# Where the last-state products of three head groups stand in a hybrid decoder layer

## The chip, the cores and the metric

The kernel runs on one core of a Trainium2 chip. The core has a matrix engine (TensorE, PE in the profile, with its weight loads as PEld), three engines for elementwise work (VectorE or DVE, ScalarE or ACT, GpSimd or POOL) and SyncE (SP), which only starts transfers here. Each engine takes its instructions from a queue of its own, in an order fixed when the program is built, and waits where an operand isn't ready. The metric is the device time of one execution in microseconds (us).

## The reference

One inference step of a layer with two halves, in float32, for 256 new prompt positions and 8 sequences of 8 sampled positions each (320 tokens, which are the columns of nearly every tile here):

```python
x = x + rms_post(W_out @ [chunkMLP(h) || SSD(h)])    # h = rms_pre(x)
x = x + rms_post(ConvFFN(rms_pre(x)))                # D_MODEL 2048, D_FF 5632
```

SSD is a state-space mixer of 32 heads in 4 groups. The prompt is handled in two chunks of 128 tokens. The state of a group after the prompt (128 state columns by 8 heads of 64) is one of the outputs, `ssm_state_prompt`, and nothing else reads it:

```python
states = einsum("bcsgn,bcsgr,bcsgrp->bcgrpn", bc, decay_states, xdt)       # one per chunk
new_states = einsum("bzcgr,bcgrpn->bzgrpn", chunk_decay, [init, *states])
states_in, final = new_states[:, :-1], new_states[:, -1]                   # final: the output
```

For each group the last state is thus a decayed state of chunk 0 plus a product of chunk 1: the tokens' B columns times the decayed inputs.

## The kernel before, in words

**Products.** Activations lie transposed, 128 features on the partitions and 320 tokens along the row. To hold float32 accuracy, each operand is split into a rounded part and a rest (`hi`, `lo`), and a product is made of three: `whi` with `xhi`, `whi` with `xlo`, `wlo` with `xhi` (`accumulate`, L141 to L143). Weights come in slabs of 512 KB: SP loads `wraw`, ACT casts it to `whi` (L128), DVE subtracts to get `wlo` (L130), with three buffers of each.

**Stages.** (1) the first norm and the projections by `w_in`, group by group, with the gated MLP and the four SSD groups beside them; (2) `w_out`, chunk by chunk, added into `acc_mix` by DVE (`chunk_out`, L234), each chunk right after the group that feeds it; (3) the second norm: the post-norm of the first half, the residual, and the pre-norm of the FFN; (4) the FFN's up and down products in eleven groups of 512 columns, with its convolution, and beside it the renewal of the sampled sequences' states (`renewals`); (5) the last norm.

**Order.** The program is written as Python generators. The work of the SSD groups and the renewals are tasks that advance to their next `yield` each time a weight slab has been used (`tick`). A scheduler then lays out each engine's queue by priority: `first()` and `high_priority` move instructions ahead, `tc.issue_after(x)` keeps them behind x. Where a task stands in the text is therefore not always where its instructions stand on an engine.

**An SSD group** (`ssd`, L774 on): `decayed(i, c)` (L818) has POOL multiply the inputs of chunk c by their decay, into tile `xde`; a product with chunk 0's B gives `s1_ps`, copied by ACT into `s1` (L835); DVE and ACT make the decay factors (`decays`, from sums `cs` that SP loads again from DRAM); `products` makes the outputs of the heads, in pairs (`y_ps`, L902); then POOL decays `s1` (L924). The inner function `final` (L927 on) makes the last state: a product of 128x512 in float32 (`fin_ps`, L929, `x1d` being chunk 1's decayed inputs), DVE's sum `s1 + ps` (L931), and the out DMA (L932). For groups 0 to 2 this is done at the end of the group, with the DMA on ACT's queue. For group 3 it is kept back in `rest`: its product and its sum are placed in the second norm, and its DMA goes out on POOL's queue.

**The second norm** (L1002 on). While the last chunk of `w_out` is being added, `squares_of` (L302) squares each of the 16 blocks of `acc_mix` as it becomes final and adds the squares up: ACT squares and POOL adds up to block 12; block 13's square goes to PSUM (`sq_ps`) and is added by DVE; blocks 14 and 15 have squares of their own. `root_table` (L271) has ACT load its table for the square root ahead of use, by a root of a constant; it stands behind the square of block 12. PE sums the squares over the partitions (`token_sums`, L282, three calls), `rsqrt_by_root` (L259) makes 1/root from the sums with one root on ACT, and `spread` (L290) brings the result into all partitions through PE. Between the sums and `spread` stands the last-state product of group 3. Behind `spread`, `unread` (L1005) issues eleven products of 128x320 whose results nobody reads.

`x1_ready` (L1038) then handles the 16 blocks in turn: DVE multiplies by the norm (L1043) and adds the residual (L1044), and `split` makes `h_hi` on ACT (L368) and `h_lo` on DVE (L369). The FFN's first `project` runs beside it, with six accumulators at a time: `ps_0` to `ps_3` in the four banks `mm`, and two more in banks of `misc`.

**The renewals** (L1150 on) begin with six empty steps, one per FFN weight slab.

Of the kernel before, what the change touches and what calls it, by code (L numbers as in the profile page):

```python
# [9 lines left out]
F32 = mybir.dt.float32  # L10
F32R = mybir.dt.float32r
I32 = mybir.dt.int32
AF = mybir.ActivationFunctionType
ALU = mybir.AluOpType
# [3 lines left out]
P = 128  # L18
# [3 lines left out]
NT = NP + NS  # L22
D = 2048
KD = D // P
# [10 lines left out]
def hybrid_step(  # L35
# [9 lines left out]
    nc = tc.nc  # L45
    act, dve, pool, pe, sp = nc.scalar, nc.vector, nc.gpsimd, nc.tensor, nc.sync
# [3 lines left out]
    cp = ctx.enter_context(tc.tile_pool(name="cp", bufs=1))  # L50
# [6 lines left out]
    def misc(name):  # L57
        return ms.tile([P, 512], F32, tag="ms", name=name)
# [6 lines left out]
    with tc.high_priority(offset=300000):  # L65
        dve.memset(ones, 1.0)

        ps = misc("early")
# [34 lines left out]
    def col(i):  # L103
        return prm[:, i:i + 1]


    def first():

        return tc.high_priority(offset=200000)
# [109 lines left out]
    acc = None  # L219
# [51 lines left out]
    def root_table(behind):  # L271

        there = tp.tile([P, 1], F32, tag="there", name="root_there", bufs=1)
        with tc.issue_after(behind):
            act.activation(there, ones[:, 0:1], AF.Sqrt)

    def token_sums(sq, ps=None, more=False):

        begins = ps is None
        ps = misc("tsum") if begins else ps  # L280
        for c, o in enumerate((0, P, NT - P)):
            ins = pe.matmul(ps[:, c:c + 1], sq[:, o:o + P], ones[:, 0:1], start=begins and c == 0, stop=not more and c == 2).ins  # L282
        sums_ins.append(ins)
        return ps if more else ps[:, 0:3]
# [18 lines left out]
    def squares_of(total, fold=False):  # L303

        one, held = [], []

        def step(nb):
            if nb < KD - 3:
                made = add_square(total, acc[:, nb, :], nb == 0)
                if nb == KD - 4:  # L310
                    root_table(made)
                return
            with first():
                if nb < KD - 2:
                    held.append(misc("sq_ps")[:, :NT])
                    act.activation(held[0], acc[:, nb, :], AF.Square)
                    return
                one.append(tp.tile([P, NT], F32, tag="sq", name="sq", bufs=2))
                if nb < KD - 1:
                    act.activation(one[-1], acc[:, nb, :], AF.Square)  # L320
                    dve.tensor_tensor(out=total, in0=total, in1=held[0], op=ALU.add)
                    if fold:
                        dve.tensor_tensor(out=total, in0=total, in1=one.pop(), op=ALU.add)
                else:
                    dve.tensor_tensor(out=one[-1], in0=acc[:, nb, :], in1=acc[:, nb, :], op=ALU.mult)
        return step, one
# [35 lines left out]
    def split(hi, lo, x, scale=None):  # L362

        if scale is None:
            act.copy(hi, x)
            dve.tensor_tensor(out=lo, in0=x, in1=hi.bitcast(F32), op=ALU.subtract)
        else:
            made = act.activation(hi, x, AF.Copy, scale=scale).ins  # L368
            dve.scalar_tensor_tensor(out=lo, in0=x, scalar=scale, in1=hi.bitcast(F32), op0=ALU.mult, op1=ALU.subtract)  # L369
            return made  # L370
# [20 lines left out]
    with ExitStack() as mctx:  # L391
# [350 lines left out]
        with tc.tile_pool(name="sd", bufs=1) as sd:  # L742
# [24 lines left out]
            def ssd(g):  # L767
# [47 lines left out]
                act.dma_start(xq_d[g], xq)  # L815

                def decayed(i, c):
                    xde = sd.tile([P, 512], F32, tag="xde", name="xde", bufs=1)  # L818
                    pool.tensor_tensor(out=by_head(xde), in0=by_head(xdt[:, c, :]),
                                      in1=dec[:, i, h0:h0 + 8].unsqueeze(2).to_broadcast([P, 8, 64]), op=ALU.mult)  # L820
                    return xde
# [9 lines left out]
                yield  # L831
                ps = misc("s1_ps")
                pe.matmul(ps, btok[:, 0, bs], x0d, start=True, stop=True)
                s1 = sd.tile([P, 512], F32, tag="s1", name="s1", bufs=1)
                act.copy(s1, ps)  # L835
                ps_cb = misc("cb_ps")
                for c in range(2):
# [86 lines left out]
                pool.tensor_tensor(out=by_head(s1), in0=by_head(s1),  # L924
                                   in1=dec[:, 2, h0:h0 + 8].unsqueeze(2).to_broadcast([P, 8, 64]), op=ALU.mult)

                def final():  # L927
                    ps = misc("fin_ps")
                    made = pe.matmul(ps, btok[:, 1, bs], x1d, start=True, stop=True)  # L929
                    yield made.ins  # L930
                    dve.tensor_tensor(out=s1, in0=s1, in1=ps, op=ALU.add)  # L931
                    (pool if g == 3 else act).dma_start(o_ssm_p[g], s1)  # L932
                    yield
                if g == 3:
                    rest.append(final())
                else:
                    for _ in final():
                        pass
                    yield

            tasks = [ssd(g) for g in range(4)]
            res = [[] for _ in range(4)]
# [59 lines left out]
            act.dma_start(o_sconv_p, pts)  # L1002
            act.dma_start(o_sconv_s, sst)

            def unread(n, behind):  # L1005

                ps = misc("unread")
                with tc.issue_after(behind):
                    for i in range(n):
                        made = pe.matmul(ps[:, :NT], res[2][0][:, i % 4, :P], res[2][0][:, i % 4, :], start=True, stop=True).ins  # L1010
                return made

            with first():
                with tc.issue_after(pd_last[-1]):
                    sums = token_sums(sq2, more=True)
                with tc.issue_after(sums_ins[-1]):
                    sums = token_sums(one[0], sums, more=True)
                with tc.issue_after(sums_ins[-1]):
                    sums = token_sums(one[1], sums)
                with tc.issue_after(sums_ins[-1]):  # L1020
                    made = next(rest[0])
                r = rsqrt_by_root(sums, 1.0 / D)
                behind = rsqrt_ins[-1]
                with tc.issue_after(behind):
                    next(rest[0])
                with tc.issue_after(made):
                    r2b = spread(r)
                unread(11, spread_ins[-1])
            sq3 = hp.tile([P, NT], F32, tag="ssq", name="sq3")


# [6 lines left out]
            def x1_ready(k0, nk):  # L1038
                for kt in range(k0, k0 + nk):
                    q, k = kt // 4, kt % 4  # L1040
                    a = acc[:, kt, :]
                    with first() if kt < 2 else tc.high_priority(offset=100000), tc.issue_after(added[0] if kt else behind):
                        dve.scalar_tensor_tensor(out=a, in0=a, scalar=col(prm_at["norm"][0] + kt), in1=r2b, op0=ALU.mult, op1=ALU.mult)  # L1043
                        added.append(dve.tensor_tensor(out=a, in0=a, in1=xr[q][:, k, :], op=ALU.add).ins)  # L1044
                        whole.append(split(hT[0][:, kt, :], hT[1][:, kt, :], a, col(prm_at["norm"][1] + kt)))
                        if k == 3 and q < 2:
                            load_x(q + 2)
            load_x(0)
# [9 lines left out]
    with tc.tile_pool(name="fp", bufs=1) as fp:  # L1058
# [91 lines left out]
        def renewals():  # L1150
# [4 lines left out]
            bsp = kept[:, 256:512].rearrange("p (h n) -> p h n", h=2)  # L1155
            bms = [kept[:, 512 + 256 * i:768 + 256 * i].rearrange("p (h n) -> p h n", h=2) for i in range(2)]
            xsp = more[:, :1024].rearrange("p (h n) -> p h n", h=2)
            yield from repeat(None, 6)

            def load(g, i):  # L1160

# [221 lines left out]
```

## Time and profile before

| what | value |
|---|---|
| time, median of 3 runs | 1777.94 us (1777.39 to 1778.95) |
| the profiled execution's own time | 1777.77 us |
| its span | 1775.7 us |
| PE busy | 1766.8 us (12234 instructions) |
| DVE busy | 1184.3 us |
| ACT busy | 798.8 us |
| POOL busy | 273.2 us |
| loaded and stored | 303.04 MB, 171 GB/s in the mean |

The profile shows one execution. Times in its timeline are microseconds from the start of the span; a row gives the start, the length, the engine, the line of the kernel, the operation, `out<-in`, the tile's size and a count, and in brackets the idle time ahead of it and the instruction that ended that. An operation of PE appears twice, once for the weights (PEld) and once for the product. A row with a count above 1 covers several instructions from the first start to the last end. In an answer about one tile or line, the three numbers between slashes are the shortest, the median and the longest of its instructions in ns.

### The profile page before, as it was taken

Reading aid. Unit: us, or ns where it says so; the run is one execution under the profiler, and the core shown is the slowest. Engines: PE = TensorE matmul, PEld = TensorE weight load, DVE = VectorE, ACT = ScalarE, POOL = GpSimd, SP = SyncE. Lnnn points to the kernel's source line nnn. Section 1 sums busy time; section 2 is a strip of 40 time slices with the busy share of each in tenths; the row PEclk is TensorE's granted clock in tenths of the full one; section 3 lists DMA queues with packets and bytes.
Section 4 is the critical chain, followed back from the end, with each engine's and each line's share of the span. In section 5 each row is a group of like instructions: output and inputs, shape, how many; then the busy total and the mean of one; then the engine's idle time right before and its main releaser. Section 6 shows DMA issues by size and latency. Waiting matters only on the chain.

```text
span 1775.7 us, 31251 instructions
## 1 busy us (share of the span) xinstructions
PE 1766.8 (100%) x12234; PEld 1743.1 (98%) x12234; DVE 1184.3 (67%) x2055; ACT 798.8 (45%) x1108; POOL 273.2 (15%) x591
## 2 busy tenths in 40 slices
PE   9999999999999999999999999999999999999998
PEld 9999999999999899999999999999999999999998
DVE  7348854656877778577966666766666575656475
ACT  7344544333545454445645434343434343433335
POOL 2003210000211101012322212021101010101004
PEclk9999999999999999999999999999999999999999
DMA  7455644445664644444556656566554444444442
GB/s 253 136 165 167 196 151 149 155 154 192 214 211 156 193 161 148 155 161 155 161 189 199 208 174 206 181 197 204 178 194 147 153 150 151 157 146 153 152 149 107
DMA packets 228498, 303.04 MB, mean 171 GB/s; under 512 B 19488, under 2 KB 150656, under 8 KB 228160
## 3 DMA queue, kind: packets, MB, share of 16 engines
q1 hardware_dynamic: 216560, 281.27, 49.5%
q10 hardware_dynamic: 10304, 15.30, 2.4%
q0 software_dynamic: 1488, 4.49, 0.8%
q8 instruction: 96, 1.57, 0.3%
q14 instruction: 50, 0.41, 0.1%
HBM read 283.44 MB, written 17.58 MB: 170 GB/s over the span
## 4 chain that ended last, share of the span: by engine, by line
PE 96%; DVE 1%; DMA 1%; ACT 1%; issue 0%; POOL 0%; SPq 0%; DVEq 0%; ACTq 0%; POOLq 0%
PE ps L141 20%; PE ps L143 20%; PE ps L142 20%; PE pd L141 10%; PE pd L142 10%; PE pd L143 10%; PE y_ps L902 1%; DMA cs<-dacs_d 1%; PE sg L708 0%; PE yo_ps L851 0%; PE up_ps L1197 0%; DMA wraw<-in_w_in 0%; PE tsum L282 0%; PE vt_ps L597 0%; PE xt_ps L380 0%
## 5 line engine op out<-in xcount | busy, mean ns | idle before, releaser
L130 DVE TENSOR_TENSOR wlo<-wraw,whi 128x1024 fp32r<-128x1024 f32 x470 | 584.6, 1244 | 384.7 <-ACT whi L128 382.0
L128 ACT CAST whi<-wraw 128x1024 fp32r<-128x1024 f32 x470 | 492.1, 1048 | 706.1 <-PE ps L142 413.4
L141 PE MATMUL ps<-h_hi,whi 128*128 128x320 f32 x2528 | 783.2, 310 | 1.3 <-DVE ev L359 0.9
L142 PE MATMUL ps<-h_lo,whi 128*128 128x320 f32 x2528 | 780.1, 309 | 0.0
L143 PE MATMUL ps<-h_hi,wlo 128*128 128x320 f32 x2528 | 779.7, 309 | 0.2 <-DVE wlo L130 0.2
L141 PEld LDWEIGHTS ps<-h_hi,whi 128*128 128x128 f32 x2528 | 474.8, 188 | 4.2 <-issue 1.8
L142 PEld LDWEIGHTS ps<-h_lo,whi 128*128 128x128 f32 x2528 | 474.9, 188 | 1.2 <-issue 0.5
L143 PEld LDWEIGHTS ps<-h_hi,wlo 128*128 128x128 f32 x2528 | 474.4, 188 | 0.6 <-DVE wlo L130 0.5
L141 PE MATMUL pd<-fhi,whi 128*128 128x320 f32 x704 | 217.3, 309 | 0.0
L143 PE MATMUL pd<-fhi,wlo 128*128 128x320 f32 x704 | 217.3, 309 | 0.0
L142 PE MATMUL pd<-flo,whi 128*128 128x320 f32 x704 | 217.3, 309 | 0.0
L141 PE MATMUL pd<-ohi,whi 128*128 128x320 f32 x448 | 139.1, 311 | 0.0
L142 PE MATMUL pd<-olo,whi 128*128 128x320 f32 x448 | 139.0, 310 | 0.0
L143 PE MATMUL pd<-ohi,wlo 128*128 128x320 f32 x448 | 138.7, 310 | 0.0
L142 PEld LDWEIGHTS pd<-flo,whi 128*128 128x128 f32 x704 | 132.2, 188 | 0.7
L143 PEld LDWEIGHTS pd<-fhi,wlo 128*128 128x128 f32 x704 | 132.2, 188 | 0.0
L141 PEld LDWEIGHTS pd<-fhi,whi 128*128 128x128 f32 x704 | 132.2, 188 | 0.0
L234 DVE TENSOR_TENSOR acc_ffn<-acc_ffn,pd 128x320 f32<-128x320 f32 x160 | 77.2, 483 | 33.3 <-PE pd L143 32.4
L141 PEld LDWEIGHTS pd<-ohi,whi 128*128 128x128 f32 x448 | 84.1, 188 | 1.0 <-issue 0.4
L142 PEld LDWEIGHTS pd<-olo,whi 128*128 128x128 f32 x448 | 84.1, 188 | 0.7 <-issue 0.4
L143 PEld LDWEIGHTS pd<-ohi,wlo 128*128 128x128 f32 x448 | 84.1, 188 | 0.2 <-issue 0.2
L1094 POOL COPY ptf<-pad 128x2 f32<-128x2 f32 x88 | 19.8, 227 | 405.2 <-DVE pad L1082 404.6
(300 smaller groups left out, 1578.6 us busy)
## 6 DMA issues: line engine op xcount, KB each, us to landing
wraw<-in_ffn_w_up SPq DMA_DIRECT2D x176, 512.0 KB, 3.5
wraw<-in_w_in SPq DMA_DIRECT2D x142, 512.0 KB, 3.5
wraw<-in_ffn_w_down SPq DMA_DIRECT2D x88, 512.0 KB, 3.3
wraw<-in_w_out SPq DMA_DIRECT2D x64, 512.0 KB, 3.3
st<-in_state_ssm SPq DMA_DIRECT2D x64, 256.0 KB, 4.3
out_ssm_state_sample<-st ACTq DMA_DIRECT2D x32, 256.0 KB, 2.6
cs<-dacs_d SPq DMA_DIRECT2D x16, 320.0 KB, 4.9
xr<-in_xT SPq DMA_DIRECT2D x4, 640.0 KB, 4.6
```

The costliest lines, as they stand in the source:

```text
L128: act.copy(hi[:, :m], raw[:, :m])
L130: dve.tensor_tensor(out=lo[:, :m], in0=raw[:, :m], in1=hi[:, :m].bitcast(F32), op=ALU.subtract)
L141: pe.matmul(ps, whi, xhi, start=first, stop=False)
L142: pe.matmul(ps, whi, xlo, start=False, stop=False)
L143: newest[0] = pe.matmul(ps, wlo, xhi, start=False, stop=last).ins
L234: dve.tensor_tensor(out=acc[:, nb, :], in0=acc[:, nb, :], in1=ps[:, :NT], op=ALU.add)
L902: pe.matmul(ps[64 * i:64 * i + 64, cols], w(hl), x(hl, m, cpx), tile_position=(0, 64 * i), **flags)
L1094: pool.tensor_copy(ptf[:, k, :], pad[:, 256:258])
```

## The change

- In groups 1, 2 and 3, `ssd` no longer makes the last state. It appends its group number, `s1`, `x1d` and a function that issues the product to `rest`, and ends without the last `yield`. Group 0 is as before. The tiles `s1` and `x1d` move to a pool that lives through the whole kernel, with three buffers each; `x1d` no longer shares the tile `xde`.
- In the second norm, group 1's product stands where group 3's stood, and ACT copies it into `x1d` (whose old content has been used). The products of groups 2 and 3 stand behind `spread`, in place of the eleven unread ones; group 3's uses a bank of `mm`. ACT copies them after the split of blocks 0 and 1.
- The sums `s1 + x1d` are written at the head of `renewals`, on POOL instead of DVE, every second of the six steps that were empty, each followed by its out DMA on ACT's queue. Nothing holds them there: in the order of the changed program the three POOL sums follow POOL's last square of the second norm, and the three out DMAs stand on ACT's queue between the copies and the splits of the first blocks.
- The root's table is loaded behind the square of block 14 instead of block 12, in the second norm alone (`fold` is set in the last norm).
- The scratch for dynamic DMAs goes from its default of 16384 to 4096 bytes.

In the order of the changed program some work next to these places moves as well: around the end of group 1 and the start of group 2, the products of one weight slab stand ahead of group 2's last `y_ps` pair instead of ahead of its first products, and SP issues the first state loads of group 3 one weight slab earlier.

```diff
--- before.py
+++ after.py
@@ -307,7 +307,7 @@
         def step(nb):
             if nb < KD - 3:
                 made = add_square(total, acc[:, nb, :], nb == 0)
-                if nb == KD - 4:
+                if nb == KD - 4 and fold:
                     root_table(made)
                 return
             with first():
@@ -317,7 +317,9 @@
                     return
                 one.append(tp.tile([P, NT], F32, tag="sq", name="sq", bufs=2))
                 if nb < KD - 1:
-                    act.activation(one[-1], acc[:, nb, :], AF.Square)
+                    made = act.activation(one[-1], acc[:, nb, :], AF.Square).ins
+                    if not fold:
+                        root_table(made)
                     dve.tensor_tensor(out=total, in0=total, in1=held[0], op=ALU.add)
                     if fold:
                         dve.tensor_tensor(out=total, in0=total, in1=one.pop(), op=ALU.add)
@@ -815,7 +817,7 @@
                 act.dma_start(xq_d[g], xq)
 
                 def decayed(i, c):
-                    xde = sd.tile([P, 512], F32, tag="xde", name="xde", bufs=1)
+                    xde = cp.tile([P, 512], F32, tag="x1d", name="x1d", bufs=3) if c else sd.tile([P, 512], F32, tag="xde", name="xde", bufs=1)
                     pool.tensor_tensor(out=by_head(xde), in0=by_head(xdt[:, c, :]),
                                       in1=dec[:, i, h0:h0 + 8].unsqueeze(2).to_broadcast([P, 8, 64]), op=ALU.mult)
                     return xde
@@ -831,7 +833,7 @@
                 yield
                 ps = misc("s1_ps")
                 pe.matmul(ps, btok[:, 0, bs], x0d, start=True, stop=True)
-                s1 = sd.tile([P, 512], F32, tag="s1", name="s1", bufs=1)
+                s1 = cp.tile([P, 512], F32, tag="s1", name="s1", bufs=3)
                 act.copy(s1, ps)
                 ps_cb = misc("cb_ps")
                 for c in range(2):
@@ -924,19 +926,14 @@
                 pool.tensor_tensor(out=by_head(s1), in0=by_head(s1),
                                    in1=dec[:, 2, h0:h0 + 8].unsqueeze(2).to_broadcast([P, 8, 64]), op=ALU.mult)
 
-                def final():
-                    ps = misc("fin_ps")
-                    made = pe.matmul(ps, btok[:, 1, bs], x1d, start=True, stop=True)
-                    yield made.ins
-                    dve.tensor_tensor(out=s1, in0=s1, in1=ps, op=ALU.add)
-                    (pool if g == 3 else act).dma_start(o_ssm_p[g], s1)
-                    yield
-                if g == 3:
-                    rest.append(final())
-                else:
-                    for _ in final():
-                        pass
-                    yield
+                if g:
+                    rest.append((g, s1, x1d, lambda ps: pe.matmul(ps, btok[:, 1, bs], x1d, start=True, stop=True).ins))
+                    return
+                ps = misc("fin_ps")
+                pe.matmul(ps, btok[:, 1, bs], x1d, start=True, stop=True)
+                dve.tensor_tensor(out=s1, in0=s1, in1=ps, op=ALU.add)
+                act.dma_start(o_ssm_p[g], s1)
+                yield
 
             tasks = [ssd(g) for g in range(4)]
             res = [[] for _ in range(4)]
@@ -1002,14 +999,6 @@
             act.dma_start(o_sconv_p, pts)
             act.dma_start(o_sconv_s, sst)
 
-            def unread(n, behind):
-
-                ps = misc("unread")
-                with tc.issue_after(behind):
-                    for i in range(n):
-                        made = pe.matmul(ps[:, :NT], res[2][0][:, i % 4, :P], res[2][0][:, i % 4, :], start=True, stop=True).ins
-                return made
-
             with first():
                 with tc.issue_after(pd_last[-1]):
                     sums = token_sums(sq2, more=True)
@@ -1017,15 +1006,19 @@
                     sums = token_sums(one[0], sums, more=True)
                 with tc.issue_after(sums_ins[-1]):
                     sums = token_sums(one[1], sums)
+                fin = [misc("fin_ps")]
                 with tc.issue_after(sums_ins[-1]):
-                    made = next(rest[0])
+                    made = rest[0][3](fin[0])
                 r = rsqrt_by_root(sums, 1.0 / D)
                 behind = rsqrt_ins[-1]
-                with tc.issue_after(behind):
-                    next(rest[0])
+                act.copy(rest[0][2], fin[0])
                 with tc.issue_after(made):
                     r2b = spread(r)
-                unread(11, spread_ins[-1])
+                made = spread_ins[-1]
+                for state in rest[1:]:
+                    fin.append(mm.tile([P, 512], F32, tag="mm", name="fin_ps") if state is rest[2] else misc("fin_ps"))
+                    with tc.issue_after(made):
+                        made = state[3](fin[-1])
             sq3 = hp.tile([P, NT], F32, tag="ssq", name="sq3")
 
 
@@ -1043,6 +1036,10 @@
                         dve.scalar_tensor_tensor(out=a, in0=a, scalar=col(prm_at["norm"][0] + kt), in1=r2b, op0=ALU.mult, op1=ALU.mult)
                         added.append(dve.tensor_tensor(out=a, in0=a, in1=xr[q][:, k, :], op=ALU.add).ins)
                         whole.append(split(hT[0][:, kt, :], hT[1][:, kt, :], a, col(prm_at["norm"][1] + kt)))
+                    if kt in (0, 1):
+                        with first(), tc.issue_after(whole[-1]):
+                            act.copy(rest[1 + kt][2], fin[1 + kt])
+                    with tc.high_priority(offset=100000):
                         if k == 3 and q < 2:
                             load_x(q + 2)
             load_x(0)
@@ -1155,7 +1152,11 @@
             bsp = kept[:, 256:512].rearrange("p (h n) -> p h n", h=2)
             bms = [kept[:, 512 + 256 * i:768 + 256 * i].rearrange("p (h n) -> p h n", h=2) for i in range(2)]
             xsp = more[:, :1024].rearrange("p (h n) -> p h n", h=2)
-            yield from repeat(None, 6)
+            for g, s1, x1d, _ in rest:
+                yield
+                yield
+                pool.tensor_tensor(out=s1, in0=s1, in1=x1d, op=ALU.add)
+                act.dma_start(o_ssm_p[g], s1)
 
             def load(g, i):
 
@@ -1371,7 +1372,7 @@
     from concourse import mybir as _mybir
     from concourse.bass_utils import run_bass_kernel_spmd as _run
 
-    nc = _bacc.Bacc("TRN2", target_bir_lowering=False, num_devices=1)
+    nc = _bacc.Bacc("TRN2", target_bir_lowering=False, num_devices=1, dynamic_dma_scratch_size=4096)
     arrays = laid_out({k: _np.asarray(v) for k, v in inputs.items()})
     args = [nc.dram_tensor(name, a.shape, _mybir.dt.from_np(a.dtype), kind="ExternalInput").ap() for name, a in arrays.items()]
     for name, shape in _OUTS:
```

## Prediction

> **What bounds the kernel now.** I read the page first (busy time per engine, then the chain that ended last), and after it the timeline of the two places where the change moves work: groups 1 and 2 of the state-space part (575 to 640 us) and the second norm (811 to 825 us).
>
> ```profile
> span 1775.7 us, 31251 instructions
> PE 1766.8 (100%) x12234; PEld 1743.1 (98%) x12234; DVE 1184.3 (67%) x2055; ACT 798.8 (45%) x1108; POOL 273.2 (15%) x591
> ...
> PE 96%; DVE 1%; DMA 1%; ACT 1%; issue 0%; POOL 0%; SPq 0%; DVEq 0%; ACTq 0%; POOLq 0%
> ```
>
> TensorE (PE) is busy for all but 8.9 us of the span, and 96% of the chain is PE. So only two things can move the end: PE work that is taken away or made longer, and waits of PE. 1766.8/12234 gives 0.144 us for a product of the common sort. The profiled execution took 1777.77 us, 2.07 more than its span and 0.17 below the median of 1777.94; the sum is made against 1777.77. A measurement of this kernel can tell 0.2% from no change, so "no change" is 1774.38 to 1781.50.
>
> **Part 1: the last-state products of groups 1 and 2 leave their places.**
>
> ```profile
> 581.10 1.12 PE L929 MATMUL fin_ps<-xde,btok 128*128 128x512 f32 x2
> 582.15 0.54 PE L902 MATMUL y_ps<-cs,xdt 128*64 128x128 f32 x5
> 585.01 0.63 PE L380 MATMUL xt_ps<-ident,x 128*128 128x128 f32 x4 [0.42 <-DVE s L931]
> ...
> 621.27 0.54 PE L902 MATMUL y_ps<-cs,xdt 128*64 128x128 f32 x5 [0.49 <-DVE cs L891]
> 622.18 1.12 PE L929 MATMUL fin_ps<-xde,btok 128*128 128x512 f32 x2
> 633.96 0.41 PE L141 MATMUL ps<-h_hi,whi 128*128 128x320 f32 x1 [0.93 <-DVE ev L359]
> 639.11 0.41 PE L143 MATMUL ps<-h_hi,wlo 128*128 128x320 f32 x1 [0.19 <-DVE wlo L130]
> ```
> ```profile
> 575.00:590.00 15.00, 14.58 (x110) 12.56 (x109) 13.51 (x34) 8.23 (x16) 3.72 (x4) 1.00 0.47 142
> 620.00:640.00 20.00, 18.39 (x136) 17.03 (x131) 14.74 (x32) 13.22 (x20) 3.12 (x3) 1.00 0.38 125
> ```
>
> In the windows the columns are length, busy time of PE, its weight loads, DVE, ACT and POOL, granted clock, DMA share, GB/s. PE's idle time in them is 15.00 - 14.58 = 0.42 and 20.00 - 18.39 = 1.61 = 0.49 + 0.93 + 0.19: the bracketed waits are all there is.
>
> - A last-state product holds PE from 581.10 to 582.15, 1.05 us, at full clock. Two go: -2.10. Nothing else of the path goes with them unless PE waits in their place.
> - The wait of 0.42 before xt_ps at 585.01 was released by the DVE sum L931 of this very state. That sum goes into the FFN: -0.42. Bounds: 0 (xt_ps waits for the next older DVE work) and -0.42.
> - The wait of 0.49 before y_ps at 621.27 is for a decay factor from DVE. In the changed program's order, the 24 products of one weight slab stand ahead of this y_ps pair that before stood earlier: 24 x 0.144 = 3.5 us more for DVE to be ready. -0.49; bounds 0 and -0.49.
> - The waits of 0.93 (ev) and 0.19 (wlo) have no edit that aims at them, but DVE has 0.69 us less to do for each of the two sums in this stretch. I take 0; bound -1.12.
> - The tiles that are kept (s1, x1d, three buffers each) end a reuse: before, the next group's copy into s1 waited for the previous out DMA. No row names that as a wait of PE: 0.
>
> Part 1: -3.0, from 0 (all that leaves comes back as waits) to -4.1.
>
> **Part 2: the second norm.** The rows of PE, DVE and ACT, from the table load to the first split blocks:
>
> ```profile
> 811.04 1.28 ACT L275 ACT_TABLE_LOAD   x1
> 812.81 1.04 ACT L128 CAST whi<-wraw 128x1024 fp32r<-128x1024 f32 x1
> 813.88 1.23 DVE L130 TENSOR_TENSOR wlo<-wraw,whi 128x1024 fp32r<-128x1024 f32 x1
> 814.46 1.39 PE L282 MATMUL tsum<-ones,sq 128*128 128x1 f32 x12
> 815.02 0.48 DVE L234 TENSOR_TENSOR acc_mix<-acc_mix,pd 128x320 f32<-128x320 f32 x1
> 815.53 0.49 DVE L325 TENSOR_TENSOR sq<-acc_mix 128x320 f32<-128x320 f32 x1
> 816.08 0.74 PEld L282 LDWEIGHTS tsum<-ones,sq 128*128 128x128 f32 x6 [0.31 <-DVE sq L325]
> 816.77 1.10 PE L929 MATMUL fin_ps<-xde,btok 128*128 128x512 f32 x2
> 817.14 0.20 ACT L264 ACTIVATE rs_s<-rs_v 128x3 f32<-128x3 f32 x1 [1.58 <-DVE rs_v L263]
> 818.12 0.81 PE L290 MATMUL spread<-ident,rs_r 128*128 128x128 f32 x3 [0.24 <-DVE rs_r L268]
> 818.58 3.23 PE L1010 MATMUL unread<-ohi 128*128 128x320 f32 x11
> 819.54 0.49 DVE L1044 TENSOR_TENSOR acc_mix<-acc_mix,xr 128x320 f32<-128x320 f32 x1
> 820.07 0.56 ACT L368 ACTIVATE h_hi<-acc_mix,prm 128x320 fp32r<-128x320 f32 x1 [2.73 <-DVE acc_mix L1044]
> 821.27 0.54 DVE L369 SCALAR_TENSOR_TENSOR h_lo<-acc_mix,prm,h_hi 128x320 fp32r<-128x320 f32 x1
> 821.39 0.56 ACT L368 ACTIVATE h_hi<-acc_mix,prm 128x320 fp32r<-128x320 f32 x1 [0.75 <-DVE acc_mix L1044]
> 823.17 1.02 ACT L368 ACTIVATE h_hi<-acc_mix,prm 128x320 fp32r<-128x320 f32 x2 [1.22 <-DVE acc_mix L1044]
> ```
> ```profile
> 818.00:819.00 1.00, 0.88 (x5) 0.91 (x6) 0.63 (x2) 0.00 (x0) 0.10 (x1) 0.60 0.01 2
> 819.00:820.00 1.00, 1.00 (x5) 1.00 (x5) 0.96 (x3) 0.00 (x0) 0.49 (x1) 0.50 0.06 16
> 820.00:821.00 1.00, 1.00 (x5) 1.00 (x5) 1.00 (x4) 0.56 (x1) 0.00 (x0) 0.50 0.69 258
> 821.00:822.00 1.00, 1.00 (x7) 1.00 (x6) 1.00 (x3) 0.56 (x1) 0.00 (x0) 0.69 0.01 4
> ```
>
> - Root table two blocks later. The cast whi at 812.81 stood behind the table load and the first use of Sqrt; it now stands ahead of both, so wlo and with it the last acc and sq on DVE start earlier. Before, the third sums started at 816.08, 0.06 after sq ended (815.53 + 0.49). Now they are held by the first twelve sums, which end about 815.8 and were not held by DVE: -0.3 on the way to spread. A later cast, between the table and the root at 817.14, leaves some 0.2 of slack; if it is lost, the gain is 0 and the root is late by up to the table's 1.28 minus that slack, about 1 us.
> - One last-state product stands at 816.77 as before, now group 1's: 0. Its DVE sum becomes an ACT copy, off the path (ACT is idle for 1.58 before 817.14, and the copy comes behind the root).
> - Unread out, two last-state products in. The eleven took 3.23, 0.29 each, twice the 0.144: the granted clock was 0.50 here, and the windows put its return to 1.00 at 821.6. At half clock a last-state product takes at most 2 x 1.05 = 2.1; I take 2.0, since not all of 1.05 need scale. They start at 818.58 - 0.3 = 818.26. Of 4.0 us at half clock, 3.36 lie before 821.62; the other 0.64 takes 0.32 at full clock. PE is free at 821.94. Before, it was free about 821.5 (818.58 + 3.23 less the overlap with spread, and the products after it up to 821.62 ran at half clock). +0.43; bounds +0.1 (1.7 each) and +0.53 (2.1 each).
> - The queues behind it. In the changed order ACT runs: copy of group 1's product, its out DMA, h_hi(0), copy of group 2's, h_hi(1), copy of group 3's, the two other out DMAs, h_hi(2), h_hi(3). The sums on POOL, though written for the FFN, stand right behind POOL's last square, so each runs as soon as its copy is there, and each out DMA holds ACT until its sum is done:
>
> ```profile
> 627.00 0.42 ACT L880 ACTIVATE cpx<-cs 128x256 f32<-128x256 f32 x1 [5.93 <-DMA cs<-dacs_d]
> 627.03 0.34 ACTq L932 DMA_DIRECT2D out_ssm_state_prompt<-s  x1
> ...
> L924 POOL TENSOR_TENSOR s<-s,dec x4: 1042/1347/1884, 492.3 to 710.1; 128x512 f32<-128x512 f32 x4
> L835 ACT COPY s<-s_ps x4: 572/586/587, 465.7 to 684.3; 128x512 f32<-128x512 f32 x4
> ```
>
>   An out DMA waited on ACT's queue behind a cpx that waited 5.93 us, and went with it: the queue is in order. A copy costs 0.57 (L835), a POOL pass over such a tile 1.04 to 1.88 (L924), a DMA's issue 0.34. Sum 1 runs 818.2 to 819.25, ahead of h_hi(0) at 819.8: 0. Sum 2 follows group 2's copy (product done 820.3, copied 820.9): 820.95 to 822.0. Group 3's copy ends about 822.5, sum 3 about 823.6, its DMA is issued about 824.0 to 824.5, and h_hi(2) ends about 825.1. From 821.94 on PE needs h_lo(0) at its 6th product (822.7), h_lo(1) at the 13th (823.8), h_hi(2) at the 27th (825.8), h_lo(2) at the 29th (826.1). So h_hi(2) is just in time. h_lo is nearer:
>
> ```profile
> 597.44 1.04 POOL L819 TENSOR_TENSOR xde<-xdt,dec 128x512 f32<-128x512 f32 x1 [10.85 <-PE s_ps L833]
> 597.51 2.06 DVE L130 TENSOR_TENSOR wlo<-wraw,whi 128x1024 fp32r<-128x1024 f32 x1 [1.25 <-ACT whi L128]
> ```
>
>   Beside a POOL pass a wlo took 2.06 instead of the 1.23 at 813.88: DVE lost 0.83 of the pass's 1.04. Sums 2 and 3 lie beside h_lo(0) and h_lo(1): h_lo(0) ends about 822.55, in time; h_lo(1) about 824.2, 0.4 late. +0.4; bounds 0 (DVE goes first) and +1.2 (a pass of 1.88).
>   [...]
> - The sums and out DMAs in the FFN, the freed software queue, the smaller scratch: 0. What hides them is PE's backlog of weight slabs, in which DVE is 67% busy; without it a sum costs 1.04.
>
> Part 2: +0.43 + 0.4 = +0.83; bounds -0.3 and +1.8. Sum: 1777.77 - 3.0 + 0.83 = 1775.6, 0.13% below the median.
>
> **The rivals.**
> - C, faster: the norm costs nothing (DVE goes ahead of POOL, the products take 1.7 at half clock), and all bracketed waits of part 1 go. 1777.77 - 4.1 + 0.1 = 1773.8. For it: DVE loses work in just those stretches. Against: no edit touches ev and wlo.
> - D, the change does not pay: the state-space part is held by the transfers of cs (5.93 at 627.00), so PE gets through sooner only to wait at the next step, and what goes is 0 to -0.42. With +0.83 that is 1778.2 to 1778.6. For it: 627.00 shows ACT waiting for cs. Against: in both windows PE's waits are small, products of weight slabs filling it; 5.93 is ACT's wait, not PE's.
> - B, slower: the clock. The granted clock fell to 0.50 at 818.2 and came back at 821.6, after PE had been busy throughout. The eleven unread products kept it busy there. If PE now has gaps between the last-state products and the first block (h_hi(0), h_lo(0), h_lo(1)) the half clock goes on for n more such stretches of 3.4 us, each costing 1.7. It ends slower than before from n = 2 (1775.6 + 3.4 = 1779.0), and by over 0.2% from n = 4 (1782.4). Against: two last-state products at half clock last longer than the eleven, and the gaps that I find are 0.4 at most. [...]
>
> **How the numbers follow.** Forecast 0.48: the products that leave are certain, the small waits and small costs around them less so; its own range is 1774.4 to 1777.2. C 0.24, D 0.19, B 0.09. The range reaches from C with half of the table's gain, 1773.3, to D with the norm's upper bound, 1777.77 + 1.8 = 1779.6; outside it stays most of B and little of C. Faster by over 0.2% is C: 0.24. Slower by over 0.2% is B from n = 4, or a late root with all upper bounds: 0.08. The rest, 0.68, is no change.
>
> **What the profile of the changed kernel would show.** Right: no L929 row of groups 1 and 2 between 575 and 640, PE's idle time there no more than 1.12, and the third group's work about 3.0 earlier. In the norm: the table load behind the cast of 812.81; the third sums about 0.3 earlier against the twelve; two last-state products of 1.9 to 2.1 at clock 0.50; a wait of about 0.4 for h_lo, none for h_hi(2). Wrong: PE waiting for cs or decay factors where the last-state products stood (D); a clock of 0.50 past two stretches (B); ACT waiting for a POOL sum while PE waits for h_hi(2), or the root late behind a cast (the norm's upper bound).

## The result and the profile after

| | before | after |
|---|---|---|
| median of 13 runs each | 1779.16 us (1776.73 to 1781.03) | 1775.17 us (1773.55 to 1776.96) |
| the profiled execution | 1777.77 us, span 1775.7 | 1774.31 us, span 1772.6 |

The ratio is 0.998, with a 95% interval of 0.9973 to 0.9987: a gain of 0.2%, as large as the bound that was called "no change". The profiled executions differ by 3.46 us, 3.1 of it inside the span. The forecast was a gain of 2.2.

The first lines of the page after:

```profile
span 1772.6 us, 31221 instructions
PE 1765.2 (100%) x12223; PEld 1740.8 (98%) x12223; DVE 1183.2 (67%) x2052; ACT 800.8 (45%) x1111; POOL 281.5 (16%) x593
...
PE 98%; DVE 1%; DMA 0%; issue 0%; SPq 0%; POOL 0%; ACT 0%; DVEq 0%; ACTq 0%
```

PE is busy for 1.6 us less and idle for 1.5 us less (7.4 after, 8.9 before), so it is not the products alone. To see where, take four instructions of PE that both programs have and compare their places: a head pair near the end of group 1, the first sums of the second norm, the FFN's first `spread`, and a product of the last norm. First the kernel before:

```profile
576.54 0.54 PE L902 MATMUL y_ps<-cs,xdt 128*64 128x128 f32 x5
...
867.21 0.49 PE L290 MATMUL spread<-ident,rs_r 128*128 128x128 f32 x3
1768.00 0.81 PE L1269 MATMUL x1p<-acc_ffn,ident 128*128 128x320 f32 x2 [0.24 <-DVE acc_ffn L1259]
```

Its first sums stand at 814.46 in the prediction. The same four after the change:

```profile
577.01 0.54 PE L904 MATMUL y_ps<-cs,xdt 128*64 128x128 f32 x5
...
809.93 2.10 PE L282 MATMUL tsum<-ones,sq 128*128 128x1 f32 x18
864.19 0.49 PE L290 MATMUL spread<-ident,rs_r 128*128 128x128 f32 x3
1765.00 0.81 PE L1270 MATMUL x1p<-acc_ffn,ident 128*128 128x320 f32 x2 [0.24 <-DVE acc_ffn L1260]
```

| stretch | before | after | difference |
|---|---|---|---|
| up to the head pair | 576.54 | 577.01 | +0.47 |
| head pair to first sums (groups 1 to 3) | 237.92 | 232.92 | -5.00 |
| first sums to the FFN's spread (the second norm) | 52.75 | 54.26 | +1.51 |
| from there on | 900.79 | 900.81 | +0.02 |

The first row is no effect of the change: that row stood at 576.38 to 578.53 in the runs below, whatever their edit, and the difference arises in the first 200 us (from 200 to 570 PE waits for nothing in any of the traces). So the whole effect sits in two stretches: -5.00 where -3.0 was forecast and +1.51 where +0.83 was.

**Groups 1 and 2 after.** Windows over the work that the prediction's two windows showed, a few us earlier here (columns as there), and the two `y_ps` pairs that had a wait of 0.49 between them:

```profile
570.00:585.00 15.00, 15.00 (x118) 13.77 (x117) 13.95 (x32) 10.63 (x20) 5.65 (x9) 1.00 0.50 160
615.00:635.00 20.00, 20.00 (x158) 19.74 (x157) 15.81 (x32) 14.46 (x21) 3.46 (x3) 1.00 0.46 141
```
```profile
618.52 0.66 PE L904 MATMUL y_ps<-cs,xdt 128*64 128x128 f32 x8
619.01 0.39 PE L904 MATMUL y_ps<-cpx,s 128*64 128x128 f32 x4
619.23 0.72 PE L904 MATMUL y_ps<-cs,xdt 128*64 128x64 f32 x12
```

PE's busy time fills both windows. The waits of 0.42, 0.49, 0.93 and 0.19 are all gone, 2.03 in sum; with the two products, 2.10, that makes 4.13. The rest is in how a wait is shown. The kernel before, around the 0.93 and the 0.19 that the prediction quotes (633.96 and 639.11):

```profile
632.72 0.31 PE L143 MATMUL ps<-h_hi,wlo 128*128 128x320 f32 x1
...
634.21 0.31 PE L142 MATMUL ps<-h_lo,whi 128*128 128x320 f32 x1
...
638.61 0.31 PE L142 MATMUL ps<-h_lo,whi 128*128 128x320 f32 x1
...
639.36 0.31 PE L141 MATMUL ps<-h_hi,whi 128*128 128x320 f32 x1
```

Products in a row start 0.147 apart, but each is shown 0.31 long, and a wait counts only from that modelled end. From 632.72 to 633.96 are 1.24, of which 0.15 are due, and the next start takes 0.25 instead of 0.15: the wait of "0.93" cost 1.09 + 0.10 = 1.2. The "0.19" cost 0.35 + 0.11 = 0.46. That is 0.27 more for each, 0.54 of the missing 0.87; the other 0.33 were not taken apart.

**The second norm after.** Rows of the timeline of PE, DVE, ACT and POOL from group 1's product to the second block, and the windows over it:

```profile
811.89 1.76 PE L930 MATMUL fin_ps<-x1d,btok 128*128 128x512 f32 x2
814.08 2.65 PE L930 MATMUL fin_ps<-x1d,btok 128*128 128x512 f32 x4
814.35 1.26 POOL L1158 TENSOR_TENSOR s<-s,x1d 128x512 f32<-128x512 f32 x1 [7.11 <-ACT x1d L1014]
814.91 1.05 DVE L1037 TENSOR_TENSOR acc_mix<-acc_mix,xr 128x320 f32<-128x320 f32 x1
816.64 1.00 PE L141 MATMUL ps<-h_hi,whi 128*128 128x320 f32 x5
817.14 2.76 POOL L1158 TENSOR_TENSOR s<-s,x1d 128x512 f32<-128x512 f32 x2 [1.53 <-ACT x1d L1041]
817.20 1.55 DVE L371 SCALAR_TENSOR_TENSOR h_lo<-acc_mix,prm,h_hi 128x320 fp32r<-128x320 f32 x1
818.44 1.83 ACTq L1159 DMA_DIRECT2D out_ssm_state_prompt<-s  x2
818.81 0.41 PE L142 MATMUL ps<-h_lo,whi 128*128 128x320 f32 x1 [1.17 <-DVE h_lo L371]
819.14 1.11 DVE L371 SCALAR_TENSOR_TENSOR h_lo<-acc_mix,prm,h_hi 128x320 fp32r<-128x320 f32 x1
```
```profile
812.00:813.00 1.00, 1.00 (x3) 0.17 (x2) 0.72 (x5) 0.39 (x2) 0.00 (x0) 0.60 0.01 2
...
815.00:816.00 1.00, 1.00 (x3) 0.47 (x2) 1.00 (x2) 0.00 (x0) 0.61 (x1) 0.69 0.00 0
...
817.00:818.00 1.00, 0.64 (x5) 0.38 (x3) 1.00 (x2) 0.75 (x3) 0.86 (x1) 1.00 0.18 66
818.00:819.00 1.00, 0.19 (x1) 0.19 (x2) 1.00 (x2) 0.35 (x1) 0.98 (x2) 1.00 0.00 0
```

DVE's passes beside the POOL sums take 1.05, 1.55 and 1.11 instead of 0.49, 0.54 and 0.54, and PE waits 1.17 for the first `h_lo` (and 0.20 for the second, at 820.30), where 0.4 at the second alone was forecast. The granted clock is at half from 812.2 to 815.6; before it was 818.2 to 821.6, 1.5 later against the first sums.

### The profile page after: what moved, and what is told of

Same layout as the page of the kernel before. It is cut to its first block, busy times and chain, and to the rows that moved or that the text cites. A ratio compares the mean times of both kernels' runs of the same rounds, so it can differ in the third digit from the quotient of the medians.

```text
span 1772.6 us, 31221 instructions
## 1 busy us (share of the span) xinstructions
PE 1765.2 (100%) x12223; PEld 1740.8 (98%) x12223; DVE 1183.2 (67%) x2052; ACT 800.8 (45%) x1111; POOL 281.5 (16%) x593
## 4 chain that ended last, share of the span: by engine, by line
PE 98%; DVE 1%; DMA 0%; issue 0%; SPq 0%; POOL 0%; ACT 0%; DVEq 0%; ACTq 0%
PE ps L141 21%; PE ps L143 21%; PE ps L142 21%; PE pd L141 10%; PE pd L142 10%; PE pd L143 10%; PE y_ps L904 1%; PE sg L710 0%; PE yo_ps L853 0%; PE up_ps L1198 0%; PE tsum L282 0%; PE xt_ps L382 0%; PE vt_ps L599 0%; DMA vf<-in_w_in 0%; PE s_ps L835 0%; PE x1p L1233 0%
```

## The experiments

Each run is read by the two stretches of the table above, head pair to first sums and first sums to the FFN's spread, from one profiled execution each. Only e1 and e8 have timing runs beside their profile. What each run changes is told below:

| run | groups 1 to 3 | second norm | stretches of half clock in the norm |
|---|---|---|---|
| before | 237.92 | 52.75 | 1 |
| e5, e6, e7 | 236.32, 236.85, 235.03 | 52.73, 52.28, 51.64 | 0, 1, 0 |
| after, e9 (the same kernel) | 232.92, 232.94 | 54.26, 53.62 | 1, 0 |
| e1, e10 (the same kernel) | 232.93, 233.57 | 51.71, 51.70 | 0, 0 |
| e2, e3, e8 | 232.98, 232.98, 232.93 | 53.67, 53.69, 53.52 | 1, 0, 0 |
| e4, e11 (the same kernel) | 232.94, 233.49 | 53.80, 53.46 | 2, 2 |

Two executions of one kernel differ by up to 0.64 in the first stretch (in e10 a wait of 0.17 for `ev` came back at 630.89), so single differences below that size are not firm there.

**What took the waits out of groups 1 and 2: e5, e6, e7.** Three parts of the change, each alone, on the kernel before: the order that follows from the missing `yield`, the DVE sums, the products. e5:

```diff
                     for _ in final():
                         pass
-                    yield
+                    if g == 0:
+                        yield
```

> The kernel before, with only the last yield of groups 1 and 2 left out, so that the tasks run one weight slab ahead as in the changed kernel; the last-state products and their DVE sums stay where they were. If the order is what took the waits away: the wait of 0.49 before y_ps goes (0.7 with its restart), and those of 0.93 (ev) and 0.19 (wlo) too, and PE is 1.9 to 2.5 us earlier by 640. If DVE's sums are the cause: those two stay, and at most 0.8 goes.

e6 and e7 put one branch ahead of the `else` of L937; e6 issues the product alone:

```diff
+                elif g:
+                    next(final())
+                    act.dma_start(o_ssm_p[g], s1)
+                    yield
                 else:
```

> The kernel before, with the last-state products of groups 1 and 2 kept, and only the DVE sums behind them left out (the two states come out without chunk 1's part). The order of PE is that of the kernel before. If the sums of 0.69 on DVE are what delays ev and wlo: the waits of 0.42, 0.93 and 0.19 go or shrink by 0.69 each, and PE is 1.3 to 1.9 us earlier by 640. If it is the order: only the 0.42 goes, and the rest stays within 0.2.

e7 keeps a DVE sum and leaves the product out:

```diff
+                elif g:
+                    dve.tensor_tensor(out=s1, in0=s1, in1=x1d, op=ALU.add)
+                    act.dma_start(o_ssm_p[g], s1)
+                    yield
                 else:
```

> The kernel before, with the last-state products of groups 1 and 2 left out and a DVE sum of the same size kept (the two states come out wrong). By the prediction's step PE is 2.1 us earlier by 640 and the four waits stay or grow, since DVE gets less time in front of them: 1.2 to 2.1 us earlier. If the waits hang on PE's products and not on DVE, they go with them: over 2.5 us earlier.

What PE waited for between 570 and 645, from the view of waits; e5, e6 and e7 in turn (total, times, longest):

```profile
PE xt_ps L380 <- DVE s L931: 0.4, 1, 0.4
PE ps L141 <- DVE ev L359: 0.2, 1, 0.2
PE ps L143 <- DVE wlo L130: 0.2, 1, 0.2
```
```profile
PE ps L141 <- DVE ev L359: 0.7, 1, 0.7
PE y_ps L902 <- DVE cs L891: 0.2, 1, 0.2
PE ps L143 <- DVE wlo L130: 0.2, 1, 0.2
```
```profile
PE ps L141 <- DVE ev L359: 1.3, 2, 0.8
```

The stretch lasts 236.32, 236.85 and 235.03 against 237.92: -1.60 by the order, -1.07 by the sums, -2.89 by the products. The order takes away the wait of 0.49 and most of that for `ev` (0.93 to 0.24), less than expected of it, for `wlo` stays. Leaving out the sums takes away the 0.42, as the prediction had it, half of the 0.49 and 0.2 of `ev`; the wait for `wlo` stays, so the sums' 0.69 on DVE is not what delays `wlo`. Without the products, the 0.42 and 0.49 go too: PE's order next to them changes, and the waits for `ev` grow to 1.3 in two. Together the three give 5.56, more than the 5.00, for the 0.42 and the 0.49 go in more than one of them. Which edit removes the wait for `wlo` in the changed kernel was not separated; e7 alone has none.

**What makes h_lo late: e1, e2, e3.** In e1 the sums and the out DMAs are held behind FFN work of their own queues (`kept_rows` are POOL's copies into `ptf`, `casts` ACT's casts of the slabs):

```diff
-                pool.tensor_tensor(out=s1, in0=s1, in1=x1d, op=ALU.add)
-                act.dma_start(o_ssm_p[g], s1)
+                with tc.issue_after(kept_rows[-1]):
+                    pool.tensor_tensor(out=s1, in0=s1, in1=x1d, op=ALU.add)
+                with tc.issue_after(casts[-1]):
+                    act.dma_start(o_ssm_p[g], s1)
```

> The changed kernel with the three POOL sums and the three out DMAs held behind FFN work of their own queues, so that the norm has neither. Theory A (the sums on POOL stretch DVE's passes, and h_lo of the first blocks comes late): DVE's residual pass takes 0.49 again instead of 1.05, h_lo of block 0 takes 0.54 instead of 1.55, and PE's waits of 1.17 and 0.20 go; with about 0.27 for each restart that is 1.8 to 1.9 us less than the changed kernel, span about 1770.7. Rival B (h_lo is late because h_hi stands behind copies on ACT): the copies stay, so the waits shrink by 0.3 at most and the span stays near 1772.4.

e2 has only the second of these two, the DMAs:

```diff
                 pool.tensor_tensor(out=s1, in0=s1, in1=x1d, op=ALU.add)
-                act.dma_start(o_ssm_p[g], s1)
+                with tc.issue_after(casts[-1]):
+                    act.dma_start(o_ssm_p[g], s1)
```

> The changed kernel with only the three out DMAs held back to the FFN; the sums stay on POOL in the norm. Theory A (DVE against POOL): h_lo of block 0 is as late as in the changed kernel, waits of about 1.2 and 0.2, span 1772.6 within 0.3. Rival B (the DMAs on ACT's queue hold h_hi): the waits fall by 0.4 to 1.4, span 1771.2 to 1772.2.

The timeline of e1, the residual pass and `h_lo` of block 0 and PE's wait for it, and the same of e2 with POOL's sums:

```profile
814.21 0.49 DVE L1038 TENSOR_TENSOR acc_mix<-acc_mix,xr 128x320 f32<-128x320 f32 x1
815.35 1.00 PE L142 MATMUL ps<-h_hi,whi 128*128 128x320 f32 x5
815.94 0.55 DVE L372 SCALAR_TENSOR_TENSOR h_lo<-acc_mix,prm,h_hi 128x320 fp32r<-128x320 f32 x1
816.54 0.41 PE L143 MATMUL ps<-h_lo,whi 128*128 128x320 f32 x1 [0.19 <-DVE h_lo L372]
```
```profile
816.50 2.78 POOL L1159 TENSOR_TENSOR s<-s,x1d 128x512 f32<-128x512 f32 x2 [1.56 <-ACT x1d L1042]
816.52 1.61 DVE L372 SCALAR_TENSOR_TENSOR h_lo<-acc_mix,prm,h_hi 128x320 fp32r<-128x320 f32 x1
818.19 0.42 PE L143 MATMUL ps<-h_lo,whi 128*128 128x320 f32 x1 [0.42 <-DVE h_lo L372]
```

e1: the norm lasts 51.71 instead of 54.26; `h_lo` takes 0.55. e2: 53.67, and `h_lo` still takes 1.61. So it is the sums on POOL against DVE, and the DMAs on ACT's queue cost PE nothing: this `h_lo` starts 6.61 behind the first sums in e2 and also in e9 (below), which has the DMAs in the norm. (The shorter wait of e2, 0.42, is PE coming later: half clock fell on the products of groups 2 and 3, which take 3.15 together where e1 and e9 show 1.88.) One case in numbers: `h_lo` of the changed kernel, at 817.20, came 0.06 behind a sum of 1.27 and took 1.55, 1.01 longer than the 0.54 of the kernel before, which has no sum beside it; 1.21 of the sum were still to run then.

In its timing runs e1 has a median of 1771.98 and a ratio of 0.9965 to the kernel before (0.9952 to 0.9977). That it is faster than the changed kernel (0.9973 to 0.9987) these intervals, which overlap, do not show; what is shown is the shorter norm, in two executions (e10 below).

e3 puts the root's table back:

```diff
-                if nb == KD - 4 and fold:
+                if nb == KD - 4:
                     root_table(made)
...
-                    if not fold:
-                        root_table(made)
```

> The changed kernel with the root's table two blocks earlier again, as before the change. By the prediction's step: the third sums wait for DVE again and everything from there comes 0.3 later, span 1772.9. Rival: what is behind waits for h_lo anyway, which comes from the same chain; then the waits of PE take up nothing and it is still 0.3. If the table's place does nothing: 1772.6.

The norm of e3 lasts 53.69; the changed kernel in another execution without half clock (e9, below) 53.62. The table's new place is worth 0.07, not 0.3. It does let DVE finish earlier, but the third sums start behind the first twelve either way (all eighteen products of the sums in one row, 2.10 long in e9 and 2.17 in e3). The 0.35 by which the two traces differ there (a last-state product 2.31 behind the first sums before, 816.77 - 814.46, and 1.96 after, 811.89 - 809.93) had another cause for the most part: ACT's square of block 12 in the kernel before, and in e7, which has the same code there and the table in the same place:

```profile
810.55 0.47 ACT L299 ACTIVATE sq<-acc_mix 128x320 f32<-128x320 f32 x1 [1.66 <-POOL sq L300]
```
```profile
808.53 0.47 ACT L299 ACTIVATE sq<-acc_mix 128x320 f32<-128x320 f32 x1 [1.38 <-DVE acc_mix L234]
```

Before, and in e5, the square waited for a POOL addition and was 0.28 later; in e6, e7 and all kernels after the change it waited for DVE alone. What decides that was not found out.

**The half clock: e9, e4, e11.** e9 is the changed kernel once more.

> The changed kernel once more, for another execution's clock. If where the stretch of half clock falls differs between executions: another place of it, or none, and from the third sums to the first blocks up to 0.7 us less; the waits of 1.2 and 0.2 for h_lo stay. If the place hangs on the program: half clock from 2.3 after the first sums again.

```profile
812.00:813.00 1.00, 0.81 (x2) 0.00 (x0) 0.70 (x5) 0.36 (x3) 0.00 (x0) 1.00 0.00 0
...
815.00:816.00 1.00, 0.48 (x2) 0.20 (x2) 1.00 (x4) 0.81 (x2) 0.00 (x0) 1.00 0.33 127
...
817.00:818.00 1.00, 0.02 (x1) 0.03 (x1) 1.00 (x2) 0.51 (x2) 0.99 (x2) 1.00 0.00 0
```

The same windows show the clock at 1.00 throughout. The norm lasts 53.62 instead of 54.26: the half clock of the first profile cost 0.64, as it does in e6 (one stretch, 52.28) against e7 (none, 51.64). The waits for `h_lo` are the same, 1.17 and 0.19; so in e9 against e1, both without half clock, the sums on POOL cost 53.62 - 51.71 = 1.91. They are all that the change costs here: e7, whose edit lies ahead of the norm, has the norm of the kernel before without half clock, and it lasts 51.64, 0.07 less than e1. (e5, without half clock too, lasts 52.73: the square of block 12 is late in it, and PE waits 0.56 for a `wlo` at 845.45.) The +1.51 of the first table compares two executions that happened to have one stretch of half clock each.

e4 is e1 without the products of groups 2 and 3 and their copies, so that nothing stands where the unread products stood:

```diff
-                for state in rest[1:]:
-                    fin.append(mm.tile([P, 512], F32, tag="mm", name="fin_ps") if state is rest[2] else misc("fin_ps"))
-                    with tc.issue_after(made):
-                        made = state[3](fin[-1])
...
-                    if kt in (0, 1):
-                        with first(), tc.issue_after(whole[-1]):
-                            act.copy(rest[1 + kt][2], fin[1 + kt])
```

> As e1, and the last-state products of groups 2 and 3 with their copies are left out (these two states come out wrong), so that PE stands idle between spread and the first block. If PE's idle time costs nothing beyond itself: the first block starts when h_hi is there, 0.3 to 0.7 us earlier than in e1. If the clock falls for it (rival B of the prediction): one more stretch of 3.4 us at 0.50, 1.0 to 1.7 later than e1.

e11 is e4 once more, as e10 is e1:

> The kernel of e4 once more (the states of groups 2 and 3 come out wrong). [...]

> The kernel of e1 once more. With no half clock, as in e1: span 1770.2 within 0.5. With a stretch of it in the norm: 0.3 to 1.2 us longer there.

e4, PE's first block and the windows:

```profile
816.10 1.97 PE L142 MATMUL ps<-h_hi,whi 128*128 128x320 f32 x6 [1.76 <-ACT h_hi L371]
```
```profile
815.00:816.00 1.00, 0.00 (x0) 0.00 (x0) 1.00 (x3) 0.51 (x1) 0.00 (x0) 0.50 0.00 0
...
820.00:821.00 1.00, 1.00 (x5) 1.00 (x5) 1.00 (x3) 0.00 (x0) 0.00 (x0) 0.50 0.84 143
821.00:822.00 1.00, 1.00 (x6) 1.00 (x5) 1.00 (x3) 0.00 (x0) 0.00 (x0) 0.58 0.98 404
```

e10 repeats e1 in the norm: no half clock, and 51.70. Its span is 1772.3 where 1770.2 was expected, longer even than the 1771.8 of e9; the 2.1 arose ahead of the norm, 1.60 of it before the head pair, where PE waits 1.0 for a `wlo`, and 0.64 in groups 1 to 3. With PE idle for 1.76, the half clock lasted twice as long, 815.0 to 821.8 in e4 and 814.4 to 821.2 in e11, and the norm took 53.80 and 53.46 against 51.71 and 51.70 in e1 and e10: less work, and 1.8 to 2.1 us more. In each of the two pairs the first block starts at the same distance from the first sums (5.6), and behind it PE waits for nothing in e4 and e11, so the difference is the clock. The products that replace the unread ones are of use twice: as work, and as cover. (Two stretches came in both executions without these products and in none of the eleven others; more executions were not taken.)

**Where else the sums could go: e8.** As e1, but with the anchor of the POOL sums at the FFN's fifth pad, in a stretch where POOL is idle (`heads` are POOL's copies from `fst` into the pads):

```diff
-                with tc.issue_after(kept_rows[-1]):
+                with tc.issue_after(heads[4]):
                     pool.tensor_tensor(out=s1, in0=s1, in1=x1d, op=ALU.add)
```

> As e1, with the three POOL sums right behind POOL's first five pads of the FFN, some 25 us after the norm, where POOL is idle for 17 us. If e1's loss of 0.31 near 905 comes from a sum that holds up a pad on POOL, it goes: PE 0.3 earlier than e1 from there. If the sums stretch the wlo passes beside them past what the backlog of slabs hides, PE waits up to 3 x 0.83 near 850 instead.

```profile
846.15 5.01 POOL L1160 TENSOR_TENSOR s<-s,x1d 128x512 f32<-128x512 f32 x3
```
```profile
860.10 0.80 PE L283 MATMUL tsum<-ones,sq 128*128 128x1 f32 x6 [1.59 <-DVE sq L301]
```

The three sums take 5.01 there, DVE's squares for the FFN's pre-norm (the end of this stretch) come late beside them (four additions 4.27, in e1 2.20), and PE waits 1.59 for the sum over them. The slabs' backlog did hide the `wlo` pass beside them (2.38, in e1 1.25), since PE waits for no `wlo` here; what it did not hide was the other chain that DVE carries. The norm stretch lasts 53.52, and the ratio to the kernel before is 0.9979 (0.9969 to 0.999): what e1 had gained is given back. e1 itself loses about 0.3 near 905, where its third sum stands ahead of a pad on POOL's queue. That the sum is the cause is not borne out: e10, e4 and e11 have it in the same place, and from the FFN's spread to the end of the span they take 908.59, 908.38 and 908.38 against e1's 908.72 and 908.41 of the changed kernel.

## Why the prediction was right or wrong

The time lay inside the range and on the side forecast. The two stretches moved by -3.49 where the sum said -2.17: both of its parts were too small, the gain by 2.0 and the cost by 0.7. That the forecast of 1775.6 came so near to the median of 1775.17 is in part luck: the two errors work against each other, and 13 runs put the median of before at 1779.16, where the prediction counted from 1777.77.

- **The products of groups 1 and 2, -2.10:** right. They are gone and nothing took their place.
- **The waits of 0.42 and 0.49:** right that they go. The 0.42 goes without the sums (e6), as argued; the 0.49 goes by the order alone (e5), as argued, and half of it goes without the sums too.
- **"The waits of 0.93 (ev) and 0.19 (wlo) have no edit that aims at them ... I take 0":** the step that failed. Both went, 1.12 as shown by the profile, and were in the bound. e5 shows that the order, not an edit aimed at them, took most of the `ev` wait: 0.93 became 0.24. What took the 0.19 stays open. The prediction looked at the moved weight slab only for the `y_ps` pair that it stands ahead of, not for what comes behind it.
- **The size of a wait:** the sum took a wait for what the bracket says. A wait among products cost 0.27 more; with what was not taken apart it is 0.87, and goes beyond the bound of -4.1.
- **Root table, -0.3:** wrong as to cause. It measured 0.07 (e3).
- **Unread out, two products in, +0.43:** the half clock, on which the whole step rested, is not fixed to that place. In the profile after it began 1.5 earlier, so that it fell on group 1's product and on `spread`, and cost 0.64; in e9 it was absent and PE stood idle 0.52 before the first block instead. Without half clock on either side the norm with the two products in place of the eleven is 0.07 longer (e1 against e7).
- **Sums beside h_lo, +0.4, bounds 0 to 1.2:** right that DVE's passes get longer beside POOL's (`h_lo` of block 0 takes 1.56 in e9 and 0.55 in e1), and mis-sized: 1.91 (e9 against e1). The prediction had sum 2 end about when PE comes to the first block, since the two products were to hold PE 1.6 past `h_hi` of block 0. In fact PE and sum 2 both start from that `h_hi` (sum 2 through a copy right behind it on ACT): in e9 the block starts at 815.80, after an idle 0.52, and sum 2 at 816.30. So the whole of a stretched `h_lo` lies behind PE's first five products. The stretched residual pass of block 0 (1.05 for 0.49) was not in the sum at all: the prediction set sum 1 at 0, for it ends ahead of `h_hi` of block 0, and did not look at DVE's pass that runs beside it.
- **The out DMAs on ACT, 0 on the path:** right (e2).
- **Rival C**, all bracketed waits go: that is what happened in groups 1 and 2, while the norm cost more than even the forecast. **Rival D** fell: no wait took the products' place, and none is for `cs`. **Rival B** did not occur, but what it feared was seen in e4 and e11: with the cover gone and PE idle for 1.76, they show one stretch more, its n = 1, at 1.8 to 2.1 against no stretch at all.

## What to carry to other kernels

Where PE is the bound and products stream at 0.147 us, count a wait by the distance between starts of the products around it, not by the bracket, and look at every wait behind a moved piece of work, not only at the one next to it. A pass on an otherwise idle POOL is not free while DVE carries the path: here three additions cost 1.91 at the head of the FFN's first blocks and 1.8 beside the squares of its pre-norm (e8 against e1), and further on in the FFN between nothing and 0.3. Work that must be done somewhere belongs where PE would idle anyway (here the norm took 51.71 and 51.70 with the two products behind `spread`, 53.80 and 53.46 without), but the wording of a program does not put it there: the sums written for the FFN ran in the norm until something on their own queue held them.

## What the runs showed that was not expected

The stretch of half clock in the norm differs between executions of one program: the changed kernel showed it from 2.3 after the first sums in one profile and not at all in another, and of the eleven profiled executions in which PE was covered seven had none there (e1, e3, e5, e7, e8, e9, e10). It lasted 3.4 us before and after the change, and 6.8, counted as two stretches, in e4 and e11; it started 2.3 (after) to 4.5 (e4) behind the first sums. What sets its start no run shows. The stretch cost 0.64 in the changed kernel. And the time before the head pair differed by up to 2.15 us between executions with the same work ahead of it (576.38 in e3, 578.53 in e6, where PE waits 1.35 for a `wlo` near 179), more than most single steps of this change: only differences between two places of one trace could tell these steps apart.
